# Turning the scan's x by a transposing transfer instead of TensorE

## The chip, the cores and the metric

The kernel runs on one core of a Trainium2 chip. The metric is the time of one execution on the device, in microseconds, as the median of several runs. Beside the times there is one profiled execution, whose span (first to last instruction) and whose instructions are read here. A core has five engines with a queue each, worked through in order: PE (TensorE, matrix products; its weight loads are shown as PEld), DVE (VectorE), ACT (ScalarE), POOL (GpSimd) and SP (SyncE, which here only issues transfers). Transfers that SP, ACT and POOL issue run on the same 16 DMA engines.

## The reference, cut to what matters

One layer of a hybrid block over 256 tokens of width 1024: a Mamba-2 scan and an attention read one normed input, their results are gated, merged and projected, and a gated FFN follows. The change is in the scan. With x after convolution and SiLU, per chunk of 128 tokens, in 8 groups of 4 heads of 64 channels:

```
Xc     = (X * dt[..., None])                      # tokens x (heads, 64)
CB     = einsum('bclgn,bcsgn->bcgls', Cc, Bc)
y_diag = einsum('bcgls,bgrcls,bcsgrp->bclgrp', CB, L, Xc)
y      = y_diag + y_off + X * d_skip
```

The projections come out with channels on partitions (x is 256 channels x 256 tokens per group), and the products of the scan need Xc with tokens on partitions. So x is turned once per group.

## The kernel before

Weights are streamed: 92 units of up to 1 MB, each loaded by one transfer from SP into one of three buffers (`load_raw`, L86), split by ACT into a high part (`hi`, L95) and by DVE into the rest (`lo`, L103), in two halves per unit with four buffers for each part, and multiplied on PE three times (high x high, high x low, low x high; L164 to L166 and L195 to L197). `next_unit` (L133) keeps the loads three units and the splits two units ahead of PE. A load waits on SP's queue until the split has left its buffer.

The first part loops over 8 groups g. A group projects B and C (`u_bc`), x (`u_x`), q and k (`u_qk`), z (`u_z`), and in turn a v unit (`u_v`) or a gate unit in four pieces (`u_gate`). Between these stand the small products, in two places:

- `small_1(g)`, behind `u_x(g)`: `s_y(g-1)`, the product `py` of the scan for the group before (L520), which reads that group's turned x (`xt`) and its decay matrix (`mx`); then the attention's scores and output, and a norm.
- `small_2(g)`, behind `u_z(g)` or in the middle of the gate unit: `s_cb(g)`, the product C times B (`pcb`, L480); `s_mx(g)`, 12 small exponentials and one wide one on ACT and a product on DVE; `s_xt(g)`, the turning of x; `s_st(g-1)`, a column sum (`stat`, L230); and the turning of the attention's probabilities (`pt_ps`, L572).

So the turned x of group g is made at `small_2(g)` and read two units later, by `py` in `small_1(g+1)`. In the last group one v unit stands between the two.

`s_xt` (L500) turns the four 128x128 blocks of x on PE into PSUM (`pxt`, L505), and one DVE product with dt takes them into `xt` (L507). `u_qk` (L425) copies q and k from PSUM into the one buffer `qkraw` on ACT (L434); POOL issues two small transfers of rows from it into `swap` (L436, L437), and DVE reads it for the rotation (L440). POOL also issues the broadcast loads of the running sums (`acsB`, L423) and of the gate's bias (L706).

The order of PE's instructions is that of the program, written out by hand. On the other engines and queues a planner lays them out in advance from when it expects each to be ready, with the program's order as priority; `tc.issue_after(x)` sets what follows behind x on x's engine. Nothing is reordered at run time: an instruction that waits holds all behind it on its queue.

Of the kernel before, what the change touches and what calls it, by code (L numbers as in the profile page):

```python
# [7 lines left out]

F32 = mybir.dt.float32
F32R = mybir.dt.float32r  # L10
I32 = mybir.dt.int32
AF = mybir.ActivationFunctionType
ALU = mybir.AluOpType
# [5 lines left out]
P = 128  # L19
T = 256  # L20
# [21 lines left out]
def block_kernel(tc, xtok_d, head_d, par_d, nf_d, con_d, rope_d, win_d, wgate_d, bg_d, watt_d, wssd_d, wout_d, wup_d, wdn_d, out_d):  # L42
    nc = tc.nc
    st = ExitStack()
    pool = lambda name, bufs=1, **kw: st.enter_context(tc.tile_pool(name=name, bufs=bufs, **kw))
    with st:
# [6 lines left out]
        ps_s = st_s.enter_context(tc.tile_pool(name="ps_s", bufs=1, space=PSUM))  # L53
        work = pool("work")


        par = const.tile([P, NPAR], F32, name="par")
        con = const.tile([P, C_ID + 7 * P + NH], F32, name="con")
        rope = const.tile([P, 2, T], F32, name="rope")

        head = const.tile([P, KD + 4 * D], F32, name="head")
        gates = head[:, KD:].rearrange("p (c n) -> p c n", c=2)
        wdt = con[:, 0:C_ID].rearrange("p (k h) -> p k h", h=NH)
        con3 = con[:, C_ID : C_ID + 7 * P].rearrange("p (a b) -> p a b", b=P)
        ident = con3[:, 0, :]
# [3 lines left out]
        sel = con[:, C_ID + 7 * P :]  # L69
        ones = const.tile([P, P], F32, name="ones")  # L70
        nc.vector.memset(ones, 1.0)
        one1 = const.tile([P, 1], F32, name="one1")
        nc.scalar.activation(one1, ones[:, 0:1], AF.Sqrt)
# [9 lines left out]
        def new_pair(name):  # L83
            return pairs.tile([P, 2, T], F32R, tag="pair", bufs=32, name=name)

# [7 lines left out]
        def split_high(raw, k0, n):  # L93
            hi = wpool.tile([P, 4, 256], F32R, tag="hi", bufs=4, name="hi")
            split_half.hi = nc.scalar.activation(hi[:, :n], raw[:, k0 : k0 + n], AF.Copy)  # L95
            return hi

        def split_half(raw, k0, n, hi=None):
            hi = hi or split_high(raw, k0, n)
            split_half.last_hi = split_half.hi_before  # L100
            split_half.hi_before = split_half.hi
            lo = wpool.tile([P, 4, 256], F32R, tag="lo", bufs=4, name="lo")
            split_half.lo = nc.vector.tensor_tensor(lo[:, :n], raw[:, k0 : k0 + n], hi[:, :n].bitcast(F32),  # L103
# [162 lines left out]
        for i in range(4):  # L266
            a, b = KD + 1024 * i if i else 0, KD + 1024 * (i + 1)
# [7 lines left out]
        flat = lambda ap: ap.rearrange("p a b -> p (a b)")  # L275
# [122 lines left out]
        S = [dict() for _ in range(NG)]  # L398
# [87 lines left out]
        def s_mx(g, behind):  # L486
# [10 lines left out]
            m2 = mx.rearrange("p h b l -> p h (b l)")  # L497
            nc.vector.tensor_tensor(m2, m2, flat(cb)[:, None, :].to_broadcast([P, 4, 3 * P]), op=ALU.mult)

        def s_xt(g):  # L500
            xs = S[g]["xs"]
            pxt = ps_s.tile([P, 2, T], F32, tag="ss", bufs=2, name="pxt")
            for c in range(2):
                for m in range(2):
                    nc.tensor.transpose(pxt[:, c, m * P : m * P + P], xs[:, m, c * P : c * P + P], ident)  # L505
            xt = S[g]["xt"] = ssp.tile([P, 2, 4, 64], F32, tag="xt", bufs=1, name="xt")
            nc.vector.tensor_tensor(xt, pxt.rearrange("p c (h d) -> p c h d", h=4),  # L507
                                    dt[:, :, 4 * g : 4 * g + 4][:, :, :, None].to_broadcast([P, 2, 4, 64]), op=ALU.mult)

        def s_y(g):  # L510
            xs, xt, mx, zt = (S[g][n] for n in ("xs", "xt", "mx", "zt"))
# [81 lines left out]
        dt = const.tile([P, 2, NH], F32, name="dt")  # L593
# [53 lines left out]
        atp = st_at.enter_context(tc.tile_pool(name="atp", bufs=1))  # L647
# [34 lines left out]
        def small_2(g):  # L682
            if g < NG:
                s_cb(g)
                if g:
                    s_mx(g, S[g]["qk_copy" if g == NG - 1 else "z_tanh"])
                s_xt(g)
            if 0 <= g - 1:
                s_st(g - 1)
                a_t(g - 1)  # L690
            if g == NG:
                s_pb(g - 2)
# [98 lines left out]
        for h in range(2):  # L791
# [5 lines left out]
            for c in range(2):  # L797
                m = half(mt[:, c], h)
# [52 lines left out]
        for f in range(NF):  # L851
# [27 lines left out]
            p = new_pair("act")  # L879
# [179 lines left out]
```

## Time and profile before

| | |
|---|---|
| median of 3 runs | 594.6 us (593.92 to 595.66) |
| the profiled execution | 594.56 us, its span 592.8 us |
| TensorE's clock granted, mean of the span | 0.996 |
| busy: PE, DVE, ACT, POOL | 98%, 77%, 63%, 4% of the span |
| mean rate of all transfers | 185 GB/s |

A row of the timeline has the start in us from the span's start, the time until the end of the last instruction in it, the engine, line, operation, written tile <- read tiles, shape and count. Matrix products overlap, and their ends are modelled; the distance from one start to the next start is the time that PE gives to one.

### The profile page before, as it was taken

To read this page: it belongs to the slowest core of one execution; us is meant where nothing else is said; L and a number is where in the kernel's file an instruction comes from. 1 tells how busy PE (TensorE), PEld (TensorE's weight loads), DVE (VectorE), ACT (ScalarE), POOL (GpSimd) and SP (SyncE) were. 2 spreads that over 40 slices of the span, in tenths; PEclk is the share of its full clock that TensorE was granted. 3 is DMA by queue.
4 is the path that set the end of the run, shared out by engine and by line. 5 is a ranking of instruction groups with operands and counts; after the bars stand their busy time and mean duration, and the time that the engine had idled before them with its cause. 6 is when DMAs were issued, how large, how long until landed. Compare 5 with 4: busy or idle time off the path is not lost.

```text
span 592.8 us, 9933 instructions
## 1 busy us (share of the span) xinstructions
PE 583.5 (98%) x3826; PEld 524.2 (88%) x3826; DVE 458.9 (77%) x891; ACT 375.9 (63%) x673; POOL 21.3 (4%) x41
## 2 busy tenths in 40 slices
PE   8999999999999999999999999999999999999994
PEld 8999999899999999999988888889888888888884
DVE  3995989888897888978896546667898898884643
ACT  2854696957768577685786343456877777774432
POOL 0010010100001000010000000000000000000100
PEclk9999999999999999999999999999999999999998
DMA  8765627662645526466245765554455546464611
GB/s 308 261 222 212 233 102 240 198 233 78 232 159 213 210 85 219 172 201 208 98 145 176 285 204 168 196 174 182 149 207 214 175 180 214 141 218 148 232 43 71
DMA packets 17936, 109.74 MB, mean 185 GB/s; under 512 B 2256, under 2 KB 2512, under 8 KB 6240
## 3 DMA queue, kind: packets, MB, share of 16 engines
q1 hardware_dynamic: 15120, 100.42, 48.2%
q0 software_dynamic: 2336, 6.85, 4.2%
q10 hardware_dynamic: 432, 1.84, 0.8%
q8 instruction: 30, 0.49, 0.3%
q14 instruction: 18, 0.15, 0.1%
HBM read 107.49 MB, written 1.08 MB: 183 GB/s over the span
## 4 chain that ended last, share of the span: by engine, by line
PE 91%; DVE 3%; DMA 3%; ACT 2%; issue 1%; DVEq 0%; ACTq 0%
PE up L174 12%; PE mm L195 10%; PE mm L196 10%; PE mm L197 10%; PE mm L164 10%; PE mm L165 10%; PE mm L166 10%; PE up L178 6%; PE py L520 2%; PE mm L293 1%; DMA acsB<-acsT_d 1%; PE po L586 1%; PE s_ps L549 1%; DVE lo L103 1%; PE mm L459 1%
## 5 line engine op out<-in xcount | busy, mean ns | idle before, releaser
L103 DVE TENSOR_TENSOR lo<-raw,hi 128x1024 fp32r<-128x1024 f32 x183 | 223.0, 1224 | 73.5 <-ACT hi L95 71.7
L95 ACT ACTIVATE hi<-raw 128x1024 fp32r<-128x1024 f32 x183 | 191.8, 1056 | 125.2 <-PE mm L197 66.4
L164 PE MATMUL mm<-hn,hi 128*128 128x256 f32 x504 | 143.6, 285 | 0.0
L165 PE MATMUL mm<-hn,hi 128*128 128x256 f32 x504 | 142.6, 283 | 0.0
L166 PE MATMUL mm<-hn,lo 128*128 128x256 f32 x504 | 142.5, 283 | 0.0
L164 PEld LDWEIGHTS mm<-hn,hi 128*128 128x128 f32 x504 | 96.7, 192 | 0.5 <-issue 0.3
L165 PEld LDWEIGHTS mm<-hn,hi 128*128 128x128 f32 x504 | 96.7, 192 | 0.2
L166 PEld LDWEIGHTS mm<-hn,lo 128*128 128x128 f32 x504 | 96.6, 192 | 0.0
L174 PE MATMUL up<-xw,hi 128*128 128x512 f32 x320 | 76.3, 391 | 0.0
L174 PEld LDWEIGHTS up<-xw,hi 128*128 128x128 f32 x320 | 58.8, 188 | 11.4
L392 DVE SCALAR_TENSOR_TENSOR cacc<-mm,par,cacc 128x255 f32<-128x255 f32 (+2 forms) x96 | 44.5, 476 | 0.7
L178 PEld LDWEIGHTS up<-xw,lo 128*128 128x128 f32 x320 | 41.0, 191 | 1.6
L178 PE MATMUL up<-xw,lo 128*128 128x256 f32 x320 | 41.5, 283 | 0.0
L196 PE MATMUL mm<-lo,act 128*128 128x512 f32 (+1 forms) x92 | 35.0, 380 | 0.0
L195 PE MATMUL mm<-hi,act 128*128 128x512 f32 (+1 forms) x92 | 34.9, 380 | 0.0
L197 PE MATMUL mm<-hi,act 128*128 128x512 f32 (+1 forms) x92 | 34.9, 380 | 0.0
L876 DVE SCALAR_TENSOR_TENSOR facc<-ab,par,facc 128x255 f32<-128x255 f32 (+1 forms) x44 | 21.3, 483 | 11.3 <-ACT facc L874 10.6
L195 PE MATMUL mm<-hi,hn 128*128 128x512 f32 x64 | 25.4, 397 | 0.0
L195 PE MATMUL mm<-hi,yn 128*128 128x512 f32 x64 | 25.2, 394 | 0.0
L197 PE MATMUL mm<-hi,hn 128*128 128x512 f32 x64 | 25.0, 390 | 0.0
L196 PE MATMUL mm<-lo,hn 128*128 128x512 f32 x64 | 25.0, 390 | 0.0
L197 PE MATMUL mm<-hi,yn 128*128 128x512 f32 x64 | 24.9, 390 | 0.0
(208 smaller groups left out, 968.0 us busy)
## 6 DMA issues: line engine op xcount, KB each, us to landing
raw<-in_win_dram SPq DMA_DIRECT2D x34, 1024.0 KB, 4.8
raw<-in_wup_dram SPq DMA_DIRECT2D x22, 1024.0 KB, 4.7
raw<-in_wdn_dram SPq DMA_DIRECT2D x10, 1024.0 KB, 4.9
raw<-in_wgate_dram SPq DMA_DIRECT2D x8, 1024.0 KB, 5.4
raw<-in_wssd_dram SPq DMA_DIRECT2D x8, 1024.0 KB, 5.0
acsB<-acsT_d POOLq DMA_DIRECT2D x8, 512.0 KB, 5.9
raw<-in_watt_dram SPq DMA_DIRECT2D x4, 1024.0 KB, 5.3
raw<-in_wout_dram SPq DMA_DIRECT2D x4, 1024.0 KB, 5.5
```

Source lines behind the costliest of these rows:

```text
L95: split_half.hi = nc.scalar.activation(hi[:, :n], raw[:, k0 : k0 + n], AF.Copy)
L103: split_half.lo = nc.vector.tensor_tensor(lo[:, :n], raw[:, k0 : k0 + n], hi[:, :n].bitcast(F32), op=ALU.subtract)
L164: nc.tensor.matmul(ps[m], wh, xh, start=a, stop=False)
L165: nc.tensor.matmul(ps[m], wh, xl, start=False, stop=False)
L166: nc.tensor.matmul(ps[m], wl, xh, start=False, stop=z)
L174: nc.tensor.matmul(ps[:, m].rearrange("p a b -> p (a b)"), hi[:, kk, m * P : m * P + P], act[k].rearrange("p a b -> p (a b)"), start=(k == ...
L178: nc.tensor.matmul(ps[:, m, 1], lo[:, kk, m * P : m * P + P], act[k][:, 0, :], start=False, stop=(k == len(tiles) - 1))
L195: nc.tensor.matmul(o, xh, wh, start=(k == 0 if apart else k0 + k == 0), stop=False)
L196: nc.tensor.matmul(o, xh, wl, start=False, stop=False)
L197: nc.tensor.matmul(o, xl, wh, start=False, stop=(k0 + k == nk - 1))
L392: nc.vector.scalar_tensor_tensor(acc[:, s:], src[:, m, : T - s], w(m, 3 - s), acc[:, s:], op0=ALU.mult, op1=ALU.add)
L876: nc.vector.scalar_tensor_tensor(acc[:, s:], src[:, : T - s], w(2 - s), acc[:, s:], op0=ALU.mult, op1=ALU.add)
```

## The change

The four PE products and their PSUM tile go. Instead, per group: POOL copies x, seen as 1024 numbers of 16 bits per partition, so that all low halves stand ahead of all high halves (`apart`), into the buffer of `xt`; SP issues one transposing transfer of these 8 blocks of 128x128 halves into a tile `turned`, which has the one buffer of `qkraw`; ACT, somewhere behind the tanh of z, joins the halves again with two copies of 512 halves per partition; and DVE multiplies by dt in place, now from SBUF.

```diff
+        def halves(t):
+            return flat(t).bitcast(U16).rearrange("p (n two) -> p two n", two=2)
+        def apart(t):
+            return flat(t).bitcast(U16).rearrange("p (two n) -> p two n", two=2)
         def s_xt(g):
             xs = S[g]["xs"]
-            pxt = ps_s.tile([P, 2, T], F32, tag="ss", bufs=2, name="pxt")
-            for c in range(2):
-                for m in range(2):
-                    nc.tensor.transpose(pxt[:, c, m * P : m * P + P], xs[:, m, c * P : c * P + P], ident)
             xt = S[g]["xt"] = ssp.tile([P, 2, 4, 64], F32, tag="xt", bufs=1, name="xt")
-            nc.vector.tensor_tensor(xt, pxt.rearrange("p c (h d) -> p c h d", h=4),
-                                    dt[:, :, 4 * g : 4 * g + 4][:, :, :, None].to_broadcast([P, 2, 4, 64]), op=ALU.mult)
+            xt2 = xt.rearrange("p c h d -> p c (h d)")
+            turned = atp.tile([P, 2, T], F32, tag="qkraw", bufs=1, name="turned")
+            nc.gpsimd.tensor_copy(apart(xt2), halves(xs))
+            nc.sync.dma_start_transpose(flat(turned).bitcast(U16).rearrange("p (a b) -> p a b", b=P), flat(xt2).bitcast(U16))
+            with tc.issue_after(S[g]["z_tanh"].ins):
+                for i in range(2):
+                    t = flat(turned).bitcast(U16).rearrange("p (i m c b) -> p i c m b", i=2, m=2, c=2)[:, i]
+                    o = flat(xt2).bitcast(U16).rearrange("p (c m b two) -> p two c m b", c=2, m=2, two=2)[:, i]
+                    nc.scalar.activation(o, t, AF.Copy)
+            nc.vector.tensor_tensor(xt, xt, dt[:, :, 4 * g : 4 * g + 4][:, :, :, None].to_broadcast([P, 2, 4, 64]),
+                                    op=ALU.mult)
```

## Rows read from the trace of the kernel before

**Rows 1.** The page: busy us (share) and instructions of each engine.
```profile
PE 583.5 (98%) x3826; PEld 524.2 (88%) x3826; DVE 458.9 (77%) x891; ACT 375.9 (63%) x673; POOL 21.3 (4%) x41
```

**Rows 2.** The page: the chain that ended last, by engine.
```profile
PE 91%; DVE 3%; DMA 3%; ACT 2%; issue 1%; DVEq 0%; ACTq 0%
```

**Rows 3.** Timeline of PE in group 4, around the turning: start, length, what.
```profile
188.54 0.60 PE L505 MATMUL pxt<-con,xs 128*128 128x128 f32 x4
188.97 0.50 PE L230 MATMUL stat<-ones,zt 128*128 128x1 f32 x4
```

**Rows 4.** Groups of instructions by line: xcount | busy us, mean ns | idle before.
```profile
L507 DVE TENSOR_TENSOR xt<-pxt,dt 128x512 f32<-128x512 f32 x8 | 5.5, 684 | 0.0
...
L526 ACT ACTIVATE zt<-yg 128x512 f32<-128x512 f32 x8 | 5.0, 631 | 3.1 <-DVE yg L525 3.1
...
L651 POOL MEMSET swap<- 128x512 f32 x2 | 1.0, 526 | 20.7 <-DVE hn L349 20.7
...
L937 POOL TENSOR_TENSOR x<-x,nfb 128x512 f32<-128x512 f32 x2 | 2.7, 1371 | 260.8 <-ACT junk L807 260.8
```

**Rows 5.** Transfers of the whole span: queue totals; issues, KB each, us to landing.
```profile
q0 software_dynamic: 2336, 6.85, 4.2%
...
raw<-in_win_dram SPq DMA_DIRECT2D x34, 1024.0 KB, 4.8
...
out_dram<-x SPq DMA_DIRECT2D x3, 256.0 KB, 2.4
```

**Rows 6.** Group 4, timelines of DVE (x ready) and POOL (row transfers out of qkraw).
```profile
175.25 0.43 DVE L396 SCALAR_TENSOR_TENSOR xs<-th,cacc 128x256 f32<-128x256 f32 x1
...
180.92 0.49 POOL L437 DMA_DIRECT2D swap<-qkraw  x1
```

**Rows 7.** Transfers issued from 182 to 186 us (group 4).
```profile
raw<-in_win_dram SPq DMA_DIRECT2D x2, 1024.0 KB, 8.0
```

**Rows 8.** Timeline of ACT in group 4.
```profile
183.46 0.58 ACT L474 ACTIVATE zt<-mm 128x512 f32<-128x512 f32 x1
...
187.46 1.04 ACT L496 ACTIVATE mx<-mx 128x1024 f32<-128x1024 f32 x1
188.40 1.99 ACT L95 ACTIVATE hi<-raw 128x1024 fp32r<-128x1024 f32 x2
```

**Rows 9.** Timeline of PE in group 4: the unit split at 188.40, and py.
```profile
195.50 0.28 PE L164 MATMUL mm<-hn,hi 128*128 128x256 f32 x1
...
207.10 1.41 PE L520 MATMUL py<-mx,xt 128*64 128x256 f32 x14
```

**Rows 10.** Group 7, timelines: row transfer, load, splits, the product py.
```profile
295.33 0.49 POOL L437 DMA_DIRECT2D swap<-qkraw  x1
...
296.78 0.33 SPq L90 DMA_DIRECT2D raw<-in_wssd_dram  x1
...
301.07 2.95 ACT L95 ACTIVATE hi<-raw 128x1024 fp32r<-128x1024 f32 x3
...
303.01 1.23 DVE L103 TENSOR_TENSOR lo<-raw,hi 128x1024 fp32r<-128x1024 f32 x1
...
304.81 1.41 PE L520 MATMUL py<-mx,xt 128*64 128x256 f32 x14
```

**Rows 11.** Transfers issued from 294 to 297 us (group 7).
```profile
swap<-qkraw POOLq DMA_DIRECT2D x2, 32.0 KB, 1.6
```

**Rows 12.** Group 1: POOL's row transfer; transfers from 78 to 82 us; PE's py.
```profile
79.09 0.49 POOL L437 DMA_DIRECT2D swap<-qkraw  x1
...
swap<-qkraw POOLq DMA_DIRECT2D x2, 32.0 KB, 2.8
...
92.70 1.52 PE L520 MATMUL py<-mx,xt 128*64 128x256 f32 x16
```

**Rows 13.** Busy us by engine in groups 1 and 7: length; PE, PEld, DVE, ACT, POOL.
```profile
66.00:94.00 28.00, 27.86 (x234) 26.55 (x232) 25.88 (x63) 21.45 (x47) 1.54 (x3) 1.00 0.52 176
283.00:306.00 23.00, 23.00 (x200) 21.78 (x198) 20.62 (x52) 18.63 (x45) 1.00 (x2) 1.00 0.29 95
```

More of the change, by code (lines that the diff above doesn't have):

```diff
@@ L9 @@
 F32 = mybir.dt.float32
+U16 = mybir.dt.uint16
 F32R = mybir.dt.float32r
```

## The prediction

> **What bounds the kernel now.** I read the page's busy shares first, then the chain, then one group on PE, then what the new chain of work has to fit beside. PE is busy 98% of the span and DVE 77%, ACT 63%, POOL 4% [rows 1]; the granted clock is full in the mean (0.996). The chain that ended last lies on PE for 91% [rows 2]. So what is taken from PE is gained, as long as nothing that PE waits for comes later than it would then want it. In the scan PE goes from one product to the next without a hole: in group 4 the four turnings start at 188.54 and the next product at 188.97 [rows 3]. The 0.60 us in that row is the modelled, overlapping length; the step from start to start, 0.43 us, is what PE gives to them.
>
> **What goes.** 8 groups of four turnings at 0.43 us: 3.44 us of PE. They waited for nothing, so no stall goes with them, and what is late next is the next product of PE's program. DVE's product with dt stays at 684 ns [rows 4]; it reads SBUF where it read PSUM, and I price that at nothing. One PSUM tile less per group only makes buffers free earlier: nothing either way, since PE did not wait there.
>
> **What comes, on engines with room.** POOL copies 1024 numbers of 16 bits per partition. The trace has no such copy. The nearest rows are a fill of 512 numbers at 526 ns and a product of two inputs over 512 at 1371 ns [rows 4]; twice those are 1.05 and 2.74 us, and I take 1.9, the middle, as a copy reads one input. ACT joins with two copies of 512 numbers per partition, 631 ns each by the row of the same size from SBUF to SBUF [rows 4]: 1.26 us a group, 10 us of an engine that idles 37%. Together with DVE's 0.68 us, 1.94 us stand between the landing of the transfer and the product `py`.
>
> **The transfer's time.** Nothing before is a transposing transfer, and its time decides the case. It moves 256 KB. Below: 2.4 us, for 256 KB issued by the same queue [rows 5]. Above: POOL's queue moved 2336 packets in 4.2% of 16 engines' 592.8 us [rows 5], 0.17 us a packet; if each run of 128 halves costs one such packet there are 1024, 64 per engine, and 10.9 us. I take 4.8 us, what the 1 MB loads need [rows 5]: small pieces should make it dearer than 2.4, but the spread over 16 engines is the same as for the loads. Both ends stay in the range.
>
> By the Trainium skill (VectorE: DVE Perf Modes, "The three transpose paths") one 128x128 block of 16 bits takes a transposing transfer 1309 ns, so by an estimate 8 in a row 10.5 us; by another page of the Trainium skill (DMA: Bandwidth & Descriptors, "Latency and other measured facts") it moves 261 GB/s and more, by an estimate about 1 us for the data. No run here shows either so far; by the first the sum would be that of the second rival, by the second the forecast.
>
> **When it can start, and when it must be there.** `turned` has `qkraw`'s buffer, so the transfer waits for POOL's two row transfers to land. x itself is done earlier: group 4 has it at 175.68, and the second row transfer is issued at 180.92 [rows 6]; at the 1.6 us that such a one took in group 7 [rows 11] it lands at 182.5. POOL's copy fits between 175.7 and 180.4; put behind the row transfers and the bias loads on POOL instead, it delays the start by some 2 us.
>
> - *Groups 2 to 6 (group 4 read).* Start 182.5, `py` at 207.10 [rows 9]: 24.6 us for a chain of 4.8 + 1.94. Hidden, with 17 us left. Odd groups have a v unit where even ones have a gate, and some 5 us less. On ACT the joins stand behind the tanh of z (end 184.04); the exponentials run until 188.5 and the splits of the next unit follow [rows 8]. If the joins follow the exponentials, they start at 188.5; the transfer should be there by 187.3, or, if it queues behind the load issued just before it (8.0 us to landing there [rows 7]), by 190.4. Then the split starts near 191.7 instead of 188.4, and PE wants that unit at 195.50 - 0.43 = 195.07 [rows 9]. A split is 1.0 us on ACT and 1.2 on DVE ([rows 8, 10]), so it may start as late as 192.8. Cost nothing; without that cover, each us more is a us of PE.
> - *Group 1.* Start 79.09 + 2.8 = 81.9, `py` at 92.70 - 0.43 = 92.27 [rows 12]. 81.9 + 4.8 + 1.94 = 88.6; nothing.
> - *Group 7.* The tight one: only the v unit lies between. Start 295.33 + 1.6 = 296.9, PE wants `py` at 304.81 - 0.43 = 304.38 [rows 10, 11]. 296.9 + 4.8 = 301.7, plus 1.94 is 303.6: in time, if ACT and DVE take it at once. But from 301.07 three splits run on ACT until 304.02 [rows 10]. Joins behind the second end at 304.2, and DVE has a split of its own on (303.01 to 304.24), so `xt` is done near 304.9; behind the third, near 306.0. Late by 0 to 1.7 us; I take 0.8.
> - *Group 0.* Nothing: x is done long before, and `py` is 15 us behind `small_2` in program order as in the others.
>
> On SP the transposing transfer stands between loads and holds those behind it while it waits. In group 4 the load before it goes at 182.4 and the next at 184.8, so the hold is short, and a load that lands some us later has the splits' lead of a unit over PE as cover. In all the transfers gain 2 MB on 110. I price SP and the DMA engines at nothing, with the upper end in the second rival.
>
> **The sum.** The profiled execution took 594.56 us, which is the median of 594.6 (its span 592.8 and 1.8 around it). 594.6 - 3.44 + 0.8 = 592.0 us.
>
> **Rivals.**
>
> 1. *The gain is paid back in the last group.* If the transfer takes 8 us (7 to 9), group 7 has 296.9 + 8 + 1.94 = 306.8 against 304.38, 2.4 us late, the others still hide it: 594.6 - 3.44 + 2.4 = 593.6, or up to 595.3 at 9 us with 0.6 us in group 1. For it: group 7's room is 7.5 us and the load issued at 296.78 [rows 10] is on the same queue just ahead. Against: the same bytes have taken 2.4 us.
>
> 2. *ACT stands waiting for the transfer, and the splits behind it with it: slower.* At 10.9 us: group 7 has 296.9 + 10.9 + 1.94 = 309.7, 5.4 us late; group 1 has 94.7, 2.5 late; in each of groups 2, 4 and 6 ACT is held from 188.5 to 182.5 + 10.9 = 193.4, the joins end at 194.7, the split with its rest on DVE at 197.0, against 195.1: 1.9 late, three times 5.7. Sum 13.6, 594.6 - 3.4 + 13.6 = 604.8 us. It decides from a transfer of about 8.5 us, where the late us equal the 3.44 gained. If the planner sets the joins straight behind the tanh, ahead of the exponentials, it is worse by up to 4.4 us in each of these groups. For it: ACT is in order, and each group's exponentials and splits lie right behind that tanh [rows 8]; the planner has never placed such a transfer in this trace, so its expectation can be far off. Against: PE's lead over the splits, 4.3 us in group 4.
>
> 3. *POOL's copy holds DVE.* DVE has 28.00 - 25.88 = 2.1 us to spare in group 1 and 23.00 - 20.62 = 2.4 us in group 7 [rows 13]. If the copy stops DVE for its whole length (1.05 to 2.74), the spare goes, and at the upper end 0.6 and 0.3 us are late there; in the other groups DVE has more room. 592.0 + 0.9 = 592.9. For it nothing in the trace, as POOL reads SBUF there only in two products at the end, with no row that shows DVE beside them.
>
> The Trainium skill (SBUF — State Buffer, "Who interferes with whom") has the rule for this rival: a DVE instruction with two SBUF inputs and a POOL instruction that reads SBUF exclude each other for a whole instruction. `lo` and most products of the scan are such; no run here shows it so far.
>
> 4. *The change doesn't take the work off PE's path*, since something else already sets the pace: 594.6. Against it, PE's row of products has no hole around any of the turnings [rows 3].
>
> **Chances.** Forecast (transfer up to 7 us) 0.46, with its own range 591.2 to 592.8. Rival 1 0.18, rival 2 0.25, rival 3 0.06, rival 4 0.05. A time within 0.3% (1.8 us) of before can't be told from no change: 592.8 to 596.4. Faster is the forecast, 0.46. Rivals 1, 3 and 4 lie within 0.3% and make 0.29; 0.03 of that I give to slower, for a displaced queue that costs what I priced at nothing, which leaves 0.26. Slower is rival 2 with that, 0.28. The range goes from 590.9 (all 3.44 us, and a little from buffers that come free earlier) to 604.8, the second rival at the upper bound of its transfer, as the unknown time reaches that far.
>
> **What would show it.** The column sum (L230) starting right behind `pcb`, with no PE hole before `py` of groups 0 to 6: the gain and the cover. The median from issue to landing of the new transfer: up to 7 us the forecast, 7 to 9 the first rival, over that the second, which would also show ACT's idle time before the joins ended by the transfer, and PE idle behind `lo`. A hole before `py` of group 7 sizes the 0.8. `lo` or other DVE products longer than their 1.2 us while POOL copies would be rival 3. The prediction is wrong if PE's products of the scan have holes in most groups, or if the planner has moved splits or loads so that a stage far from `s_xt` changes its length.

## The result, and the profile after

The change made the kernel slower: 604.0 us median of 10 runs (599.05 to 610.18) against 594.0 of 10 runs before (593.65 to 597.85), ratio to before 1.0137 with a 95% interval of 1.0100 to 1.0175. Measured a second time, it took 597.8 (593.33 to 603.52, 7 runs) against 594.4, ratio 1.0042 [1.0011, 1.0072]. The forecast was 592.0. From a quarter to seven tenths of the executions of most kernels here, the one before too, are some 3 to 5 us longer than the rest, so a kernel's lowest times are given beside its median, and the ratios leave out the executions far above the others of their kernel (610 and 603.5 us here; in the experiments 715 us of one version and 2915 us of the kernel before).

The profiled execution took 599.05 us (span 597.3), 4.5 more than the one before; its page answers to [rows 1, 2]. From the page: busy time by engine, granted clock in 40 slices, the chain.

```profile
PE 582.9 (98%) x3794; PEld 523.0 (88%) x3794; DVE 461.0 (77%) x891; ACT 385.7 (65%) x689; POOL 29.6 (5%) x49
...
PEclk9999999999999999998999999999999999999998
...
PE 78%; ACT 7%; DMA 6%; DVE 6%; issue 2%; POOL 0%; SPq 0%; DVEq 0%; ACTq 0%
```

32 products fewer, and PE as busy: 582.9 us against 583.5. PE's share of the chain falls from 91% to 78%; ACT, DMA and DVE, 8% together before, have 19%, and one slice of the clock is at 8.

Transfers of the whole span (issues, KB each, median us from issue to landing), which answer to [rows 5]:

```profile
raw<-in_win_dram SPq DMA_DIRECT2D x34, 1024.0 KB, 5.2
...
turned<-xt SPq DMA_TRANSPOSE x8, 5.9
```

The median, 5.9, is inside the 7 us that I had called the forecast's. The single ones are 3.7, 5.7, 7.2, 6.3, 6.0, 5.8, 10.6 and 4.1 us for groups 0 to 7. Each was issued while a 1 MB load stood ahead of it on SP's queue, and in seven groups it landed 0.9 to 1.2 us behind that load: in group 4 the load at 190.8 and the transfer at 192.0. In group 6 it landed 3.8 us behind, at 269.1 after 265.4:

```profile
raw<-in_win_dram SPq DMA_DIRECT2D x1, 1024.0 KB, 8.8
head<-in_bg_dram POOLq DMA_DIRECT2D x1, 256.0 KB, 7.3
turned<-xt SPq DMA_TRANSPOSE x1, 10.6
```

(These are the issues from 256.5 to 259 us; `head` is the gate's bias.) So much of the time to landing is that of the load ahead, as read from the landings; no version moves that load alone. What they cost stands in the waits of the scan (28 to 330 us: total, times, longest):

```profile
ACT xt L521 <- DMA turned<-xt: 11.6, 4, 5.8
...
DVE xt L522 <- ACT xt L521: 10.1, 3, 5.4
...
PE mm L167 <- DVE lo L104: 3.6, 2, 3.2
...
PE py L535 <- DVE ry L222: 1.3, 1, 1.3
...
PE pt_ps L587 <- ACT pr L579: 1.0, 1, 1.0
```

ACT waits for the transfer, DVE for ACT, PE for DVE's `lo`. The longest of each is one chain, in group 6. (`ry` is a small product that stands right behind `xt` on DVE, so PE's wait for it is group 7's wait for `xt`; the wait for `pr` is group 1's and has nothing to do with the transfer.) ACT there (start, length, what, in brackets the wait before it):

```profile
262.35 1.04 ACT L96 ACTIVATE hi<-raw 128x1024 fp32r<-128x1024 f32 x1
269.22 1.39 ACT L521 ACTIVATE xt<-turned 128x512 uint16<-128x512 uint16 x2 [5.83 <-DMA turned<-xt]
```

DVE there:

```profile
270.70 0.69 DVE L522 TENSOR_TENSOR xt<-xt,dt 128x512 f32<-128x512 f32 x1 [5.44 <-ACT xt L521]
...
271.38 1.22 DVE L104 TENSOR_TENSOR lo<-raw,hi 128x1024 fp32r<-128x1024 f32 x1
```

PE there:

```profile
269.17 0.28 PE L166 MATMUL mm<-hn,hi 128*128 128x256 f32 x1
272.65 0.58 PE L167 MATMUL mm<-hn,lo 128*128 128x256 f32 x1 [3.20 <-DVE lo L104]
```

For 5.83 us ACT does nothing, and the next split behind the joins waits with them. DVE stands for 5.44 us before its product with dt, and the next `lo` waits in order behind that product, although the high part that it needs was done on ACT at 263.4. When the transfer lands, joins, DVE's product and that `lo` run one behind the other, and PE steps from 269.17 to 272.65 in place of 0.12 us on: 3.4 us lost. Behind the hole its products come at 0.21 us (16 in 3.4 us) instead of 0.12. The same stretch by windows (length; busy us of PE, PEld, DVE, ACT, POOL; granted clock; DMA share; GB/s):

```profile
269.20:272.60 3.40, 0.25 (x3) 0.04 (x1) 1.90 (x5) 3.38 (x6) 0.00 (x0) 0.98 0.77 316
272.60:276.00 3.40, 3.35 (x16) 3.35 (x17) 3.40 (x8) 2.81 (x4) 0.00 (x0) 0.51 0.36 80
276.00:280.00 4.00, 4.00 (x36) 4.00 (x35) 3.17 (x7) 1.23 (x2) 0.00 (x0) 1.00 0.78 283
```

After 3.4 us in which PE worked 0.25, the granted clock is 0.51, its lower level of 1.2 GHz, for 3.4 us: half of that, 1.7 us, is lost on top. So in this execution group 6 alone loses 5 us, more than all 8 groups gain.

The account, by how much later `py` starts than before [rows 9, 10, 12]; the kernel before had it in group 6 at:

```profile
281.64 0.65 PE L520 MATMUL py<-mx,xt 128*64 128x256 f32 x4
```

and the changed kernel in groups 1, 4, 6 and 7 at:

```profile
93.11 1.09 PE L535 MATMUL py<-mx,xt 128*64 128x256 f32 x10
...
206.96 1.30 PE L535 MATMUL py<-mx,xt 128*64 128x256 f32 x12
...
285.54 1.52 PE L535 MATMUL py<-mx,xt 128*64 128x256 f32 x16
...
309.67 1.52 PE L535 MATMUL py<-mx,xt 128*64 128x256 f32 x16 [1.35 <-DVE ry L222]
```

Groups 1, 4, 6 and 7 stand at +0.4, -0.1, +3.9 (281.64 before) and +4.9 us. Taken together from the holes: this execution began the scan 0.4 late; the turnings give 8 x 0.43 = 3.44; group 1 loses 0.8, group 2 0.7, group 6 5.0, group 7 1.4: 0.4 - 3.4 + 7.9 = 4.9, of which the end keeps 4.5. Group 1's 0.8 is not the transfer's: PE waits there for ACT's `pr` in the versions without the transfer's lateness too (below).

### The profile page after: what moved, and what is told of

Same layout as the page of the kernel before. It is cut to its first block, busy times and chain, and to the rows that moved or that the text cites. A ratio compares the mean times of both kernels' runs of the same rounds, so it can differ in the third digit from the quotient of the medians.

```text
span 597.3 us, 9933 instructions
## 1 busy us (share of the span) xinstructions
PE 582.9 (98%) x3794; PEld 523.0 (88%) x3794; DVE 461.0 (77%) x891; ACT 385.7 (65%) x689; POOL 29.6 (5%) x49
## 4 chain that ended last, share of the span: by engine, by line
PE 78%; ACT 7%; DMA 6%; DVE 6%; issue 2%; POOL 0%; SPq 0%; DVEq 0%; ACTq 0%
PE up L175 12%; PE mm L196 9%; PE mm L198 9%; PE mm L197 9%; PE mm L167 7%; PE mm L165 7%; PE mm L166 7%; PE up L179 6%; DMA turned<-xt 3%; DVE lo L104 2%; PE py L535 1%; DVE cacc L393 1%; ACT hi L96 1%; PE mm L294 1%; ACT mx L494 1%
## 5 line engine op out<-in xcount | busy, mean ns | idle before, releaser
L104 DVE TENSOR_TENSOR lo<-raw,hi 128x1024 fp32r<-128x1024 f32 x183 | 223.0, 1226 | 64.2 <-ACT hi L96 62.7
L891 DVE SCALAR_TENSOR_TENSOR facc<-ab,par,facc 128x255 f32<-128x255 f32 (+1 forms) x44 | 21.2, 483 | 11.3 <-ACT facc L889 10.6
```

Of the source, the lines that this page charges most:

```text
L891: nc.vector.scalar_tensor_tensor(acc[:, s:], src[:, : T - s], w(2 - s), acc[:, s:], op0=ALU.mult, op1=ALU.add)
```

## The experiments

The theory after the result: the transfer starts behind `qkraw`'s row transfers, just where a 1 MB load and, in the even groups, the gate's bias are moved, lands after ACT has reached the joins, and all that stands behind them on ACT is late, and on DVE all behind the product with dt. Each version is compared with the kernel before, run beside it; none was run beside the changed kernel, whose ratio was 1.0137 and 1.0042 in its two measurements. Rivals: the transfer is slow of itself, by its small pieces; POOL's copy holds DVE; the reordering on ACT does it without the wait; the gain was never there.

**The tile in a buffer of its own**, so that the transfer can start with x:

```diff
-            turned = atp.tile([P, 2, T], F32, tag="qkraw", bufs=1, name="turned")
+            turned = work.tile([P, 2, T], F32, tag="ab", bufs=2, name="turned")
```

> The changed kernel, with a buffer of its own (two, taken from a tag that only the FFN uses) for the transposing transfer's target, which had the one buffer of qkraw. The transfer no longer waits for POOL's row transfers out of qkraw and can start when POOL's copy is done, some 5 to 9 us earlier in each group, ahead of the load that it queued behind. Theory (ACT, in order, is held by joins whose transfer lands late, the splits behind it come late, PE has holes, and its clock halves for a stretch behind a long hole): the transfers land before the tanh of z, no ACT wait on the transfer over 1 us, no PE hole over 1 us in groups 2 to 6, group 7 in time too, no stretch at half clock; 590.0 to 592.0 us. Rival A (the transfer's many small packets delay the weight loads, wherever it starts): the packets are the same, so 598 to 604 us with loads late. Rival B (POOL's copy holds DVE): the copies are the same, 598 to 604 us.

Measured: 594.9 us median, 591.79 to 598.11, ratio 0.9989 [0.9957, 1.0021]; five of 12 runs from 591.8 to 592.2, where before's lowest is 593.6. Its trace (592.18): transfers of the span, then ACT in group 6, then PE's largest wait of the scan.

```profile
turned<-xt SPq DMA_TRANSPOSE x8, 3.1
```

```profile
261.70 0.76 ACT L521 ACTIVATE xt<-turned 128x512 uint16<-128x512 uint16 x1
```

```profile
PE pt_ps L587 <- ACT pr L579: 1.3, 1, 1.3
```

The same 256 KB land in 3.05 to 3.8 us, 6 to 14 us before the joins in groups 1 to 7, and no hole is left in groups 2 to 7. The loss was the lateness, and the slowness was the place: with no load ahead of it the transfer takes 3.05 us. The profiled execution is inside the theory's 590 to 592 us but for 0.2; the median is not, and by it a gain is not shown. This ratio's interval overlaps that of the changed kernel's second one (1.0011 to 1.0072), so the cure rests on the trace more than on the times.

**The wait taken away, the transfer left as it is**: it reads a spare copy, and the joins read a constant, so this version leaves the turned x out of the scan.

```diff
-            nc.gpsimd.tensor_copy(apart(xt2), halves(xs))
-            nc.sync.dma_start_transpose(flat(turned).bitcast(U16).rearrange("p (a b) -> p a b", b=P), flat(xt2).bitcast(U16))
+            source = work.tile([P, 2, T], F32, tag="ab", bufs=2, name="source"); nc.gpsimd.tensor_copy(apart(source), halves(xs))
+            nc.sync.dma_start_transpose(flat(turned).bitcast(U16).rearrange("p (a b) -> p a b", b=P), flat(source).bitcast(U16))
...
-                    t = flat(turned).bitcast(U16).rearrange("p (i m c b) -> p i c m b", i=2, m=2, c=2)[:, i]
+                    t = ones.bitcast(U16)[:, None, None, 0:P].to_broadcast([P, 2, 2, P])
```

> The changed kernel, with the transfer kept as it is (from a spare source, into the same buffer behind the same waits) but the joins on ACT reading a tile of ones instead of what it brings, so that nothing waits for it; the scan's product is then of other numbers. Theory (the wait of ACT's joins is the loss): no PE hole over 1 us, 590.0 to 592.5 us. Rival A (the transfer's packets delay the loads): the packets are there as before, 597 to 604 us. Rival B (POOL's copy holds DVE): the copy is there as before, 597 to 604 us.

Measured: 592.3 us median of 10 runs, lowest 591.60, ratio 0.9960 [0.9925, 0.9994]. Transfers issued from 255 to 260 us, and ACT in group 6:

```profile
turned<-source SPq DMA_TRANSPOSE x1, 11.3
```

```profile
262.05 1.39 ACT L521 ACTIVATE xt<-ones 128x512 uint16<-128x512 uint16 x2
263.30 0.82 ACT L589 ACTIVATE pt<-pt_ps 128x384 f32<-128x384 f32 x2
264.03 1.99 ACT L96 ACTIVATE hi<-raw 128x1024 fp32r<-128x1024 f32 x2
```

The transfer is as late as ever (11.3) and nothing minds it; PE's one hole is that in group 1, before `pt_ps` (1.9 us). The joins stand one split earlier on ACT than in the changed kernel, ahead of the copies into `pt` and of the splits. So the transfer does its harm by the wait, and not by its traffic, by its hold of SP's queue or by the mere place of the two joins on ACT.

**A plain transfer of the same bytes in its place** (this version leaves the turning out):

```diff
-            nc.sync.dma_start_transpose(flat(turned).bitcast(U16).rearrange("p (a b) -> p a b", b=P), flat(xt2).bitcast(U16))
+            nc.sync.dma_start(flat(turned).bitcast(U16), flat(xt2).bitcast(U16))
```

> The changed kernel, with the transposing transfer replaced by a plain one of the same 256 KB between the same tiles, on the same queue behind the same waits; x is then not turned. 128 pieces of 2 KB take the place of 1024 packets of 256 bytes. If the lateness is that of the start and of the queue behind a 1 MB load: it lands 5 to 10 us after issue in groups 2, 4 and 6 as well, and the time stays at 596 to 604 us. If it is that of the small packets: 2.4 to 4 us, no ACT wait over 1 us, 590 to 593 us.

Measured: 599.2 us median (596.73 to 604.06, 9 runs), ratio 1.0066 [1.0035, 1.0097]. Its transfers of the span, then those issued from 263.5 to 266 us in group 6, then two windows of group 4:

```profile
turned<-xt SPq DMA_DIRECT2D x8, 256.0 KB, 5.6
```

```profile
raw<-in_win_dram SPq DMA_DIRECT2D x1, 1024.0 KB, 7.7
head<-in_bg_dram POOLq DMA_DIRECT2D x1, 256.0 KB, 6.7
turned<-xt SPq DMA_DIRECT2D x1, 256.0 KB, 6.3
```

```profile
198.90:202.00 3.10, 1.61 (x11) 1.28 (x11) 2.27 (x3) 3.10 (x4) 0.00 (x0) 1.00 0.03 12
202.00:205.50 3.50, 3.50 (x19) 3.50 (x19) 3.50 (x9) 2.11 (x4) 0.00 (x0) 0.51 0.66 222
```

In this place a plain transfer is nearly as late, with holes of 2.1 and 1.0 us in group 2, 1.1 and 1.0 in group 4, and a stretch of half clock from the second hole of each pair on. So the small pieces are not needed for the loss. They are not cleared of it either: in group 6, where the changed kernel lost 5 of its 7.9 us, the plain transfer landed 0.6 us behind the load ahead of it (271.9 after 271.2) instead of 3.8, and PE had no hole. The four profiles with the transposing transfer in this place and the bias in group 6 have 2.9 to 4.1 us there. Why it needs these 3 us more in that group, and not in groups 2 and 4, is open.

**The gate's bias loads moved to the odd groups**, everything else in the changed kernel's order:

```diff
-            if g % 2 == 0:
-                cols = slice(256 * g, 256 * g + 512)
-                for c in range(2):
+            if g % 2 or g == 0:
+                cols = slice(256 * (g + g % 2), 256 * (g + g % 2) + 512)
+                for c in range(2 if g < 7 else 0):
```

> The changed kernel with the two broadcast loads of the gate's bias (256 KB each, from POOL) moved one group ahead, from groups 2, 4 and 6 to groups 1, 3 and 5; the order on PE, DVE, ACT and SP is the same as in the changed kernel. If the bias loads, which compete with the transfer and with the 1 MB load ahead of it on SP's queue, make the even groups the late ones: there the transfer lands 5 to 6.5 us after issue, ACT waits under 1 us for it, no hole in 2, 4 and 6, 593 to 596 us. If it is the queue behind the 1 MB load alone: it takes 6 to 10 us as before, 597 to 604 us.

Measured: 597.3 us median (594.47 to 599.56, 10 runs), ratio 1.0021 [0.9997, 1.0045]. Transfers issued in group 5 (now with bias) and in group 6 (now without):

```profile
raw<-in_win_dram SPq DMA_DIRECT2D x2, 1024.0 KB, 9.3
head<-in_bg_dram POOLq DMA_DIRECT2D x1, 256.0 KB, 6.1
turned<-xt SPq DMA_TRANSPOSE x1, 8.7
...
raw<-in_win_dram SPq DMA_DIRECT2D x1, 1024.0 KB, 5.4
...
turned<-xt SPq DMA_TRANSPOSE x1, 4.4
```

The slowness went with the bias: 8.5, 9.4 and 8.7 us in groups 1, 3 and 5, and 5.2, 3.7 and 4.4 in 2, 4 and 6. The 1 MB load ahead slows too, and in every group the transfer lands 0.9 to 1.4 us behind it, group 6 included (263.5 after 262.5). The odd groups bear it, since ACT reaches their joins later (it waits 1.2 us at most); in the even ones the holes behind the joins are gone. One of 1.3 us, before `mm` for `lo`, stands in group 2 ahead of that group's transfer, and what made it is open. The median misses the 593 to 596 us of the theory and lies where the other answer had it; the profiled execution, 594.47, is this version's fastest. So the trace shows what the bias does to the transfer, and the times do not show that moving it pays.

The Trainium skill (DMA: Bandwidth & Descriptors, "Queues, rings and completion order") says that each DMA engine takes packets from the queues that have work for it in turn; the trace fits that, as SP's loads and the transposing transfer get slow together when POOL's bias loads run (9.3 and 8.7 against 5.4 and 4.4 us).

**The joins later on ACT**, behind a split of the next group, the tile still in `qkraw`'s buffer:

```diff
-            with tc.issue_after(S[g]["z_tanh"].ins):
+            S[g]["join"] = (xt, xt2, turned)
+        def s_join(g):
+            xt, xt2, turned = S[g]["join"]
+            with tc.issue_after(split_half.hi.ins if g in (2, 4, 6) else S[g]["z_tanh"].ins):
...
-                u_x(g)
+                s_join(g - 1); u_x(g)
...
-                small_2(g)
+                small_2(g); s_join(g)
```

> The changed kernel with the same transfer, started at the same place and as late as there, but with the joins of groups 2, 4 and 6 set on ACT behind two more units of splits (three splits and the gate's tanh later), and traced behind the next group's first unit in the others. Theory (the late transfer costs by what stands behind the waiting join on ACT): the transfers still take 5 to 11 us, but no PE hole in groups 2, 4 and 6 and no half clock; group 7 stays late by 1 to 2 us; 592 to 594 us. Rival A (the packets delay the loads): 597 to 604 us as in the changed kernel.

Measured: 593.8 us median (592.98 to 599.58, 12 runs), ratio 0.9996 [0.9964, 1.0028]. In its trace the transfers are as slow (up to 10.0 us), and groups 2 to 6 have no hole. The profiled execution took 596.65, with holes of 1.0 us in group 0 and of 1.2 and 1.95 in group 1, and group 7 keeps its 1.6 us. So in groups 2 to 6 the later place of the joins, and with it of DVE's product, cures what the buffer cures, without making the transfer faster; in group 7 it does not.

**Both remedies.** 

> Both remedies: the transfer's target has buffers of its own, so that it starts behind POOL's copy, and the joins stand later on ACT as in the kernel with later joins. Theory: nothing waits for the transfer by either, so the second adds nothing to the first: 590.0 to 592.5 us, as with the own buffer alone; group 1's hole before the turned probabilities (1.5 us, for ACT's exponentials) may shorten, as the joins stand behind the copies of the turned probabilities. Rival A: 597 to 604 us.

Measured: 595.8 us median of 12 runs, lowest 591.91, ratio 0.9989 [0.9959, 1.0018]: nothing over the buffer alone (0.9989, lowest 591.79), as the theory had it; its 590.0 to 592.5 us was met by the five lowest runs and missed by the median. Group 1's hole did not shorten: PE stands 1.2 and 1.95 us there, as with the later joins alone. The two profiles also show what the clock makes of one and the same hole. Windows of both remedies, then of the later joins alone (596.65):

```profile
80.70:84.40 3.70, 0.99 (x6) 0.48 (x5) 2.90 (x7) 2.99 (x10) 0.99 (x2) 0.90 0.65 126
84.40:90.50 6.10, 6.09 (x28) 5.87 (x29) 5.77 (x18) 6.10 (x16) 0.52 (x1) 0.50 0.46 167
```

```profile
80.30:84.00 3.70, 1.00 (x6) 0.48 (x5) 2.90 (x7) 2.99 (x10) 0.98 (x2) 1.00 0.29 60
84.00:90.00 6.00, 5.91 (x48) 5.72 (x49) 5.77 (x18) 6.00 (x16) 0.40 (x1) 1.00 0.74 210
```

In both PE works 1.0 of 3.7 us, in the same six products. Behind it the clock is at 0.50 in the one, for 6.8 us, and full in the other: 28 products against 48 in some 6 us.

**The turnings left out of the kernel before** (DVE reads x as it lies):

```diff
-            pxt = ps_s.tile([P, 2, T], F32, tag="ss", bufs=2, name="pxt")
-            for c in range(2):
-                for m in range(2):
-                    nc.tensor.transpose(pxt[:, c, m * P : m * P + P], xs[:, m, c * P : c * P + P], ident)
-            nc.vector.tensor_tensor(xt, pxt.rearrange("p c (h d) -> p c h d", h=4),
+            nc.vector.tensor_tensor(xt, xs.rearrange("p c (h d) -> p c h d", h=4),
```

> The kernel before, without the four turnings on PE per group; DVE multiplies x by dt as it is, so x is not turned. It measures the gain that the prediction counted: 8 x 0.43 = 3.44 us. Theory (the gain is real, and was lost again by waits): 590.2 to 591.0 us. Rival C (something else sets the pace in the scan anyway): 593.5 to 594.5 us.

Measured: 591.7 us median of 12 runs, ratio 0.9961 [0.9933, 0.9989]; profiled 591.64 against 594.56, so 2.9 of the 3.44 us; the time is a little above the theory's 590.2 to 591.0. PE in its group 1:

```profile
80.07 0.84 PE L572 MATMUL pt_ps<-con,pr 128*128 128x128 f32 x3 [0.69 <-ACT pr L564]
```

With four turnings fewer PE asks for the attention's probabilities before ACT has them: 0.7 us of waiting in group 1, which the kernel before doesn't have.

**POOL's copy added to the kernel before**, into a spare tile:

```diff
-            xs = S[g]["xs"]
+            xs = S[g]["xs"]; spare = work.tile([P, 2, T], F32, tag="ab", bufs=2, name="spare"); nc.gpsimd.tensor_copy(flat(spare).bitcast(U16).rearrange("p (two n) -> p two n", two=2), flat(xs).bitcast(U16).rearrange("p (n two) -> p two n", two=2))
```

> The kernel before, which turns x on PE, with POOL's copy of x into 16 bit halves added (into a spare tile that nothing reads). It measures what POOL's copy costs by itself. Theory (the copy is off the path): 593.5 to 594.5 us as before, DVE's products beside a copy no longer than elsewhere. Rival B (the copy holds DVE): DVE products with two SBUF inputs that overlap the 1.04 us of a copy take up to 1 us longer, PE waits in groups 1 and 7, 595 to 597 us.

Measured: 594.5 us median of 10 runs, ratio 1.0002 [0.9971, 1.0033]. The copy of group 1 on POOL, the split on DVE beside it, and the same split in the kernel before:

```profile
75.48 1.04 POOL L501 COPY spare<-xs 128x1024 uint16<-128x1024 uint16 x1 [15.19 <-DVE xs L396]
```

```profile
75.95 1.65 DVE L103 TENSOR_TENSOR lo<-raw,hi 128x1024 fp32r<-128x1024 f32 x1
```

```profile
76.75 1.22 DVE L103 TENSOR_TENSOR lo<-raw,hi 128x1024 fp32r<-128x1024 f32 x1
```

A copy takes 1.04 us and does hold DVE: this `lo`, the one split that meets a copy, is 0.4 us longer, and each of the other copies makes one DVE product beside it 0.2 to 0.4 us longer (`qk` of group 0 0.99 us instead of 0.69, small steps of the softmax 0.32 to 0.53 instead of 0.16). The mean of all 183 `lo`, 1226 ns against 1224, hides it. In the changed kernel the same split takes 1.80 us. PE has no hole from it: the hold is real, below the 1 us of the rival, and costs no time that could be seen.

**Own buffer, and group 0's probabilities turned later**, to fill the hole in group 1; and the same move in the kernel before, as control:

```diff
-                a_t(g - 1)
+                None if g == 1 else a_t(g - 1)
...
-                u_x(g)
+                u_x(g) if g != 2 else (a_t(0), u_x(g))
```

> The changed kernel with the transfer's destination in a buffer of its own (as in e1), and with the turning of group 0's attention probabilities moved from group 1's small stage to behind group 2's masks product, so that TensorE no longer stands 1.5 us in group 1 for ScalarE. Theory (lateness of the transfer was the cause of the loss, and group 1's gain is lost to ScalarE's pr): no hole over 1 us before the last group, the 1.53 us of e1 at 79.4 gone; an undisturbed run takes 592.2 - 1.0 to 1.5 = 590.7 to 591.2 us, pst starts that much earlier than in e1; ratio to before about 0.995 among undisturbed runs. Rival (the hole in group 1 is made by the whole chain of ScalarE work, so that TensorE stands a little later instead): 592.0 to 592.4, with a hole of over 1 us behind 79 us.

> The kernel before with the same move of group 0's turned attention probabilities, nothing else. Theory: in the kernel before TensorE's four turnings per group cover most of the same wait in group 1, so the move is worth at most 0.5 us: 593.1 to 593.9 in an undisturbed run. Rival (the move is worth the same with and without the transposing transfer): 592.4 to 592.9, and then e9 owes nothing of its lead over this kernel to group 1.

Measured: 591.7 us median (591.09 to 597.32, 12 runs), ratio 0.9964 [0.9938, 0.9990]; the control 594.5 (593.61 to 596.59, 12 runs), ratio 0.9995 [0.9978, 1.0013]. The move alone is worth nothing that shows. Once more, with the version unaltered:

> The version with its own buffer and group 0's turned probabilities moved, unaltered, for a second profiled execution (the first, 595.01 us, was 3.7 above the lower cluster of 591.1 to 591.8). Theory: 591.1 to 591.8 with no hole over 1 us in groups 1 to 7, pst 0.4 to 1 us earlier than the 368.84 of the version with its own buffer alone. Rival: holes at 60 and 105 us as in the first, and then these belong to this order, not to the execution.

Measured: 595.4 us median (591.13 to 597.92, 10 runs), ratio 0.9990 [0.9954, 1.0026]. The two profiled executions took 595.01 and 594.51 and have the same holes, so the second's rival holds for them. PE in the first:

```profile
105.69 0.28 PE L166 MATMUL mm<-hn,hi 128*128 128x256 f32 x1
108.44 0.39 PE L167 MATMUL mm<-hn,lo 128*128 128x256 f32 x1 [2.47 <-DVE lo L104]
```

The hole in group 1 is gone (`stat` at 80.28, the next product at 80.64), and one of 2.75 us has come in group 2, beside one of 1.0 us at 62.7, which the two versions with later joins have too. The lowest times of this version (591.1 to 591.3) lie 0.6 us below the own buffer's and 2.5 below those of before (593.6 to 593.8), but 11 of its 22 executions took 594.5 to 597.9, and no profile shows whether those at 591 have the 2.75 us too. It is faster than the kernel before by the first comparison, by 0.4%, and is not told from it by the second.

**The changed kernel a second time.** 

> The changed kernel, unaltered, for a second profiled execution: the first took 599.05 us, the lowest of ten, and has one hole of 3.48 us with a half-clock stretch of 3.4 us behind it, in group 6. Theory (the lateness of the transfer in the even groups, and nothing else, makes the spread up to 610): an execution nearer to the median has such a hole in more of groups 2, 4 and 6, each over 2 us and ending behind lo or hi, with about 5 us for one that halves the clock (3.4 and 1.7); so 599 with one, 604 with two, 609 with three. Rival (the longer executions are longer elsewhere, as all kernels have some): 604 us with one hole only, and the rest of the time in other stages.

Measured: 597.8 us median; the profiled execution, 596.76, has, beside group 1's, three smaller holes: 1.34 us in group 2, 2.05 in group 6, 1.65 in group 7. ACT's wait for the transfer in group 6 is 4.36 us. PE there, then two windows:

```profile
269.69 0.28 PE L166 MATMUL mm<-hn,hi 128*128 128x256 f32 x1
271.74 0.39 PE L167 MATMUL mm<-hn,lo 128*128 128x256 f32 x1 [1.77 <-DVE lo L104]
```

```profile
269.60:271.70 2.10, 0.37 (x3) 0.17 (x1) 1.92 (x5) 2.10 (x5) 0.00 (x0) 1.00 0.04 18
271.70:275.00 3.30, 3.26 (x27) 3.27 (x28) 3.30 (x8) 2.92 (x5) 0.00 (x0) 1.00 0.31 67
```

The transfer took 9.2 us here instead of 10.6. The hole is 1.4 us shorter, the clock stays full behind it, and 27 products fit in 3.3 us where 16 did in 3.4. My count by holes (599, 604, 609) doesn't fit: three holes make 596.8. What fits better is the clock of the whole span: 0.998 here without a half-clock stretch in the scan, 0.994 in the first profile with one of 3.4 us, 0.990 in the plain transfer's with two, 0.991 with both remedies and one of 6.8 us; the runs of the first ten over 603 us had 0.986 to 0.991. That these had longer or more such stretches is inferred; none of them was profiled, and why the first measurement had more is open.

## Why the prediction was wrong, step by step

- *What goes, 3.44 us:* right for TensorE; `stat` follows `pcb` without a hole. Of it 2.9 us reach the end when nothing is put in its place. I read the room in group 1 from `py` and missed that ACT's `pr` was just in time there.
- *POOL 1.9, joins 1.26, DVE 0.68 us:* 1.04, 1.39 and 0.69, not far off in size.
- *The transfer, 4.8 us:* 3.05 alone, 3.7 to 10.6 in its place, inside the bounds of 2.4 and 10.9. But that 10.6 meets the 10.9 is luck: the upper bound stood on small packets alone, while the transfer landed right behind the 1 MB load ahead of it, and a plain one needed 5.6 in the median. The estimate that I drew from the Trainium skill (VectorE: DVE Perf Modes, "The three transpose paths"), 10.5 us for 8 blocks in a row, does not hold: 8 take 3.05 us with no load ahead of them.
- **The step that failed: "Groups 2 to 6 (group 4 read). Start 182.5 ... Cost nothing", with "I price SP and the DMA engines at nothing".** I read one group, used the whole span's median for the transfer, and let the deadline (a landing by 187.3 to 190.4) rest on both. In group 4 the row transfers landed at 185.8, the new one started at 186.0 and landed at 192.0; in group 6 it started at 258.6 and landed at 269.1, joins and split came behind it, and PE stood 3.4 us. SP was not free either: in group 4 a 1 MB load that went at 169.6 before goes at 179.3 in the changed kernel, and the row transfers, which landed at 182.6 before, land behind it (185.4), so the start moved by 3.5 us. And a row that I quoted spoke against 4.8: the 1 MB loads needed 8.0 us in just that stretch [rows 7]. Queued behind such a load is the case that I named and gave 190.4; group 4 had it, at 192.0, and its split still came in time.
- *Group 7, 0.8 us late:* 1.4, inside 0 to 1.7, by the course that I had described (joins behind a second split on ACT, `xt` behind a split on DVE). The row transfers took 3.4 us there, not the 1.6 of before.
- *Rival 1*, the gain paid back in the last group: no, that is 1.4 us of 7.9.
- *Rival 2* is the mechanism that decided: ACT waiting for the transfer, the splits behind it late; in group 6 the split that PE waited for stood behind the wait on DVE, with its high part long done. I had the holes in groups 2, 4 and 6 at 1.9 us each, and groups 1 and 7 at 2.5 and 5.4. Measured in the two profiles: 0.7 and 1.3 in group 2, none in 4, 3.4 and 2.0 in 6, none from the transfer in 1. That its 604.8 is near the 604.0 measured is luck: it takes the transfer as slow in all groups and the clock as full, and the second measurement gave 597.8.
- *The clock* stood in no term: the hole of 3.4 us in group 6 cost 5.1 in the first profile, and the one of 2.0 in the second cost no clock.
- *Rival 3*, POOL holding DVE: as a cost refuted by the copy alone, 1.0002, though the hold is there (1.65 us for a split instead of 1.22). The trace agrees with the rule of the Trainium skill that I had put beside it (SBUF — State Buffer, "Who interferes with whom"); the hold shows no cost in this kernel. That the kernel before had no row of it was a miss of mine: beside POOL's product at 554.07 its `lo` at 554.99 takes 1.45 us.
- *Rival 4*, no gain at all: refuted, 2.9 us are there.

## What to carry to other kernels

When work goes from the bound engine to a transfer, take its time from the stretch in which it will run, among the transfers issued there, and hold each group's landing against that group's own deadline; a median over groups hides the one that decides. Look also at what stands ahead of it on its queue: it landed about 1 us behind the load issued before it in most groups. What waits for it in order matters more than its length: with the waiting instruction behind the next splits, the same slow transfer cost nothing in groups 2 to 6. A buffer shared to save space is also a start time: with one of its own the transfer started 7 to 9 us earlier in groups 2 to 6 and took 3.05 us.

## What the runs showed of the hardware that I had not expected

- A transposing transfer of 256 KB takes 3.05 us alone. Behind a 1 MB load under way on its queue it landed some 1 us after that load (0.9 to 1.2 us in seven of 8 groups): after 3.7 to 6.3 us without bias loads from POOL's queue under way, and after 4.7 to 11.3 with them.
- A plain transfer of the same bytes in the same place is hardly faster (median 5.6 against 5.9), but for group 6 (6.3 against 10.6).
- A POOL copy that reads SBUF held one DVE instruction beside it by 0.2 to 0.6 us (a split of 1.22 us took 1.65 and 1.80), while the copy kept its 1.04 us.
- TensorE's clock fell to 0.51 for 3.4 us behind 3.4 us with 0.25 busy, and behind 3.1 us with 1.61 busy, but stayed at 1.00 behind 2.1 us with 0.37 busy. Behind 3.7 us with 1.0 busy, in the same products, it fell to 0.50 for 6.8 us in one execution and stayed full in another; so the busy share of the hole alone doesn't tell what the clock does.
